# Order of the steps within a scan chunk, and the queue of the last group's norm, in a two-layer gated-MLP and state-space decoder

## The chip, the cores and the metric

One Trainium2 chip; the program runs on one core. The core has five engines with a queue each, worked off in order: TensorE (PE; its weight loads are shown as PEld), VectorE (DVE), ScalarE (ACT), GpSimd (POOL) and SyncE (SP), which only issues DMAs. ScalarE and GpSimd can issue DMAs from their own queues as well. Engines wait for each other through semaphores, and an instruction that waits holds all that stand behind it in its queue. The metric is the device time of one execution in microseconds, less is better.

## What is computed

Two layers on 1024 tokens of width 1024, in float32. Layer 0 is a chunked causal spatial-gating MLP, layer 1 a Mamba-2 mixer with 8 groups, 4 heads each, and chunks of 128 tokens. Only layer 1 matters here:

```python
def ssd_mixer(h, w_in, conv_w, conv_b, dt_bias, a_log, d_skip, norm_w, w_out):
    proj = h @ w_in                                  # z, x, B, C, dt
    xbc = silu(causal_depthwise_conv(xbc, conv_w, conv_b))        # 4 taps along tokens
    dt = softplus(dt_raw + dt_bias); dA_cs = cumsum(dt * -exp(a_log), axis=2)   # inside a chunk
    decay = exp(where(causal, dA_cs[l] - dA_cs[s], -inf))
    w_ls = einsum('bclgn,bcsgn->bclsg', Cm, Bm)[..., None] * decay * dt
    y_diag = einsum('bclsgj,bcsgjp->bclgjp', w_ls, x)             # inside a chunk
    states = einsum('bclgn,bclgj,bclgjp->bcgjpn', Bm, decay_to_end * dt, x)
    prev = scan(lambda carry, s: carry * chunk_decay + s)         # from chunk to chunk
    y = y_diag + einsum(Cm, prev, exp(dA_cs)) + x * d_skip
    gated = rmsnorm_per_group(y * silu(z), norm_w)                # over 256 channels of a group
    return gated @ w_out
# h = h + ssd_mixer(rmsnorm(h)); out = rmsnorm(h, final_norm_w)
```

## The kernel before

Large matrix products are done by a seven-product scheme (products 1 to 7 of half-size blocks), each operand split into a high and a low part so that three matmuls (`mm3`, L134 to L136) make one precise one. ScalarE makes the high part (a cast, L111), VectorE or GpSimd the low part (L112).

**The scan** (`scans`) walks over 64 chunks in the order of groups, eight of each group. Of chunk c, class `Scan` has these steps:

- `load` (SyncE): the running decays of the chunk. `decay` (ScalarE): four Relu and one Exp make the decay matrix in tile `wl` (L1544, L1546).
- `pe_a` (TensorE): transposes of x and B and the product of B and C, into the PSUM tile `tp`. `tokens`: VectorE scales x (L1552) and masks the product (L1554), ScalarE copies B (L1556, behind VectorE's two), GpSimd makes the weighted x (L1557).
- `weights` (VectorE, L1562): decay matrix times the masked product, in `wl`.
- `pe_b` (TensorE): the chunk's output `yy` (L1571 with `wl`, L1575 with the state) and its contribution `sp` to the state (L1582).
- `update` (VectorE, L1601): the state takes `sp` in. `out` (VectorE L1613, L1616, GpSimd L1619): the output is assembled. `carry` (GpSimd, L1592): the next state is decayed. `gate` (GpSimd, L1623): times silu(z).

The loop runs these staggered: in turn n it does `pe_b`, `update`, `out`, `gate` of chunk n, `weights` and `carry` of n+1, `pe_a`, `decay`, `tokens` of n+2 and `load` of n+3. PSUM tiles `tp`, `yy` and `sp` share four buffers in turn.

Between `pe_b` and `pe_a`, and at the end of the turn, `project` lets TensorE do a unit or more of other work: the input projections of groups 2, 4, 6 and 7 (PSUM tile `ab`, two buffers), then z of group 7, and from the last chunks on the first of the output products (`bo`). A finished projection puts its convolution into `queue`: a ScalarE step (L1287) and three taps on VectorE (L1281) which read `ab`, then Silu; `drain()` takes one entry per turn, and all but the newest are drained before another accumulator is taken. GpSimd makes the low part of the projections' weights (L112).

**The output product** (`bo`, class `Out`) takes its inner order 1, 2, 7, 6, 4, 5, 3. The gated outputs of groups 0 to 6 come back from DRAM (`ya<-g_d`, L1696) and are scaled with the norm's 1/rms (`rb`, read back as a broadcast, L1688; the scaling is L1701, called `ready`); group 7 stays on chip. `prep` splits the operands of one of four steps c. `hook_b(n, c)` is called ahead of the matmuls of product n, step c, and issues loads and the VectorE operations between the products. In the scan's last seven chunks `ready` and `prep` of product 1 come at the head of each turn.

**The norm of a group**: squares on ScalarE (L1634), a sum on GpSimd (L1641), row sums on TensorE (L1647), a copy (L1651), a store `sum_c` (L1654), a read-back as columns (`sv`, L1663), the inverse root in three parts `guess` (L1667, L141), `tail` (L150 to L153) and `put` (a store, L1676), and then the broadcast read `rb`. For the last group this is done by halves of the tokens (`end["half"]`). The DMAs of all groups go by SyncE's queue but for those of the last group, and `put` and `rb` of the last two, which go by ScalarE's.

All is scheduled by hand: the order of the program is the order in each queue. DMAs of SyncE and ScalarE use nine completion semaphores in turn.

Of the kernel before, what the change touches and what calls it, by code (L numbers as in the profile page):

```python
# [15 lines left out]
P = 128  # L16
# [6 lines left out]
G = 8  # L23
# [6 lines left out]
def kernel(  # L30
# [21 lines left out]
    nc = tc.nc  # L52
    x = x[0]
    out = out[0]
# [497 lines left out]
    for gp in range(G // 2):  # L552
# [4 lines left out]
        if gp == 1:  # L557
# [9 lines left out]
            for h in range(2):  # L567
# [9 lines left out]
                for k in range(4):  # L577
                    g = h * 4 + k
# [79 lines left out]
    class Out:  # L658
# [111 lines left out]
        def get(self, kind, i, k, c):  # L770

            at = kind, i, k, c if kind == "a" else c // 2
            if at not in self.had:
                self.had.add(at)
                (self.load_a if kind == "a" else self.load_b)(*at[1:])
# [569 lines left out]
    queue = []  # L1345

    def drain(n=1):

        for _ in range(min(n, len(queue))):
            for f in queue.pop(0):  # L1350
                f()
# [139 lines left out]
    ss_d = dr.tile([G, T], F32, name="ss_d")  # L1491
    rs_d = dr.tile([G, T], F32, name="rs_d")
# [16 lines left out]
    class Scan:  # L1509
# [141 lines left out]
                nc.scalar.copy(out=self.sr[h * 64:h * 64 + 1], in_=pr[h * 64:h * 64 + 1, 0:256])  # L1651

        def sum_c(self, th):
            (nc.sync if self.g < G - 1 else nc.scalar).dma_start(out=ss_d[self.g, th * 512:(th + 1) * 512].rearrange("(h t) -> h t", h=2),  # L1654
                              in_=self.sr[0:65:64])

    def group_rstd(g, t0, n):


        c = n // P  # L1660
        sv = tiny([P, 8], "sv")[:, 0:c]
        queue = nc.sync if g < G - 1 else nc.scalar
        queue.dma_start(out=sv, in_=ss_d[g, t0:t0 + n].rearrange("(p c) -> p c", c=c))  # L1663
        got = []

        def guess():
            nc.vector.tensor_scalar(sv, sv, 1.0 / 256, NORM_EPS, ALU.mult, ALU.add)  # L1667
            got.append(rsqrt_a(sv, c))

        def tail():  # L1670
            rv = tiny([P, 8], "rvv")[:, 0:c]
            rsqrt_b(rv, sv, got[0], c)
            got.append(rv)

        def put():
            (nc.sync if g < G - 2 else nc.scalar).dma_start(out=rs_d[g, t0:t0 + n].rearrange("(p c) -> p c", c=c), in_=got[1])  # L1676

        return guess, tail, put

# [3 lines left out]
    def weights(g, th):  # L1683

        if (g, th) not in rbs:
            n = min(2 - g % 2, G - 1 - g) or 1
            t = q4([P, 2, 512], "rb")
            (nc.sync if g < G - 2 else nc.scalar).dma_start(out=t[:, 0:n], in_=rs_d[g:g + n, th * 512:(th + 1) * 512].partition_broadcast(P))  # L1688
            for k in range(n):
                rbs[g + k, th] = t[:, k]  # L1690
        return rbs[g, th]
# [15 lines left out]
    def accs_b(n):  # L1707
        if n == 1:
# [3 lines left out]
    bo = Out(gd, b_w_out, gscale, lambda t, nb: h1_d[t][:, nb * 512:(nb + 1) * 512], accs_b, False,  # L1712
             (1, 2, 7, 6, 4, 5, 3))
    end = {}

    def hook_b(n, c):

        last, get = end["scan"], bo.get
        at = n, c
        if at == (1, 0):  # L1720
            for k in (2, 3):
                get("a", 0, 0, k)
            get("b", 0, 0, 2)
        elif at == (1, 2):
            for k in (0, 1):
                get("a", 0, 1, k)
            get("b", 1, 0, 0)
        elif at == (1, 3):
            end["half"] = [group_rstd(G - 1, 0, 512)]
            get("a", 0, 1, 2), get("b", 1, 0, 2)  # L1730
            for k in (0, 1):
                get("a", 1, 0, k)
            get("b", 0, 1, 0)
            end["half"][0][0]()
            last.sum_b(n=2)
        elif n == 2:
            if c == 0:
                last.sum_c(1)
                for k in (2, 3):
                    get("a", 1, 0, k)  # L1740
                get("b", 0, 1, 2)
                end["half"][0][1]()
            elif c == 1:
                end["half"][0][2]()
                end["half"].append(group_rstd(G - 1, 512, 512))
                get("a", 1, 1, 0), get("a", 1, 1, 1)
                get("a", 0, 1, 3)
                end["half"][1][0]()
            elif c == 2:
                end["half"][1][1]()  # L1750
            elif c == 3:
                end["half"][1][2]()
                bo.ready(1, 1, 0)
            if c < 2:
                bo.b12_plus(1, c)
            bo.ready(1, 0, c)
            bo.plus(bo.a(0, 0, c), bo.a(1, 0, c))
        elif n == 7:
            if c == 0:
                get("a", 1, 1, 2), get("a", 1, 1, 3)  # L1760
            if c < 3:
                bo.ready(1, 1, c + 1)
                bo.sums(2, c)
        elif n == 6:
            if c == 0:
                bo.sums(2, 3)
            bo.sums(6, c)
            if c % 2 == 0:
                get("b12", 0, 1, c)
            if c == 0:  # L1770
                end["fnwb"] = q4([P, D], "fnwb")
# [31 lines left out]
    def scans():  # L1803
# [13 lines left out]
        def project(upto):  # L1817
            while ran[0] < upto:
                next(fl, None)
                ran[0] += 1  # L1820

        def want(at):
            if at < M:
                return AHEAD + (total - AHEAD) * at // M
            return total + min(16 * (at - M) // (N - 5 - M), 16 + 2 * (at - N + 5))

        def at(f, n, *a):
            if 0 <= n < N:
                g, c = chunks[n]
                if g not in scan:  # L1830
                    scan[g] = Scan(g, nc.gpsimd)
                getattr(scan[g], f)(c, *a)
# [16 lines left out]
        for n, (g, c) in enumerate(chunks):  # L1849
            if n == M + 3:  # L1850
                drain(len(queue))
            elif n == N - 9:
                for k in range(2):
                    bo.get("a", 0, 0, k)
            elif n == N - 7:
                end["scan"] = scan[G - 1]
                bo.get("b", 0, 0, 0)
            if n >= N - 7:
                k = n - N + 7
                if k % 2:  # L1860
                    bo.prep(1, k // 2)
                else:
                    bo.ready(0, 0, k // 2)
            p = g if c >= 4 else g - 1
            at("pe_b", n, scan[p] if c % 4 == 3 and p >= 0 else None)
            project(want(n + .5))
            at("pe_a", n + 2)
            at("update", n)
            at("out", n)
            if n > 0:  # L1870
                at("weights", n + 1)
            at("decay", n + 2)
            at("carry", n + 1)
            at("tokens", n + 2)
            at("gate", n)
            drain()
            at("load", n + 3)
            th = 0 if c >= 4 else 1
            if p >= 0:
                sc = scan[p]  # L1880
                if p == G - 1:
                    if c == 5:
                        sc.gate_half(th), sc.squares(th)
                    elif c == 6:
                        sc.sum_a()
                elif c % 4 == 0:
                    sc.squares(th)
                elif c % 4 == 1:
                    sc.store(th)
                    sc.sum_a()  # L1890
            if c % 4 == 0 and n >= 8:
                scan[g - 1].sum_c(1 - th)
            if g > 0:
                if c == 5:
                    rs[g] = group_rstd(g - 1, 0, T)
                elif c == 6:
                    rs[g][0]()
                elif c == 7:
                    rs[g][1]()
            if c == 0 and g > 1:  # L1900
                rs[g - 1][2]()
            if c == 1:
                prefetch(g, 1)
            if c == 5 and g < G - 1:
                prefetch(g + 1, 0)
            project(want(n + 1))
        sc = scan[G - 1]
        sc.sum_c(0), rs[G - 1][2]()
        sc.gate_half(1), sc.squares(1)
        for _ in fl:  # L1910
            pass

# [51 lines left out]
```

## Time and profile before

| | |
|---|---|
| median of 3 runs | 1591.79 us (1590.07 to 1592.04) |
| profiled execution | 1599.45 us, its span 1597.6 us |
| mean granted clock of TensorE | 0.975 |
| busy share of the span | PE 94%, VectorE 67%, ScalarE 49%, GpSimd 26% |
| scan: first and last yy | 1071.5 us, 1425.2 us |

The profile is of one execution. A row of an order in time gives start, duration, engine, line, operation, tiles written and read, and in brackets how long the engine was idle before it and what ended the wait. `SPq` and `ACTq` rows are issues of DMAs. Waits are summed as "engine, tile, line <- what ended the wait: sum, times, longest". Weight loads and matmuls overlap, so the same wait of TensorE is a little longer when seen at the weight loads.

### The profile page before, as it was taken

The page shows a single profiled execution, that of the slowest core. Times are in us where ns is not written, and L with a number is a line of the kernel's source. Part 1 is how long each engine was busy: PE and PEld are TensorE (multiplying, and loading weights), DVE is VectorE, ACT ScalarE, POOL GpSimd, SP SyncE. Part 2 cuts the span into 40 slices and gives each one's busy share as a digit, 9 for nine tenths or more (in the row PEclk, how much of TensorE's full clock was granted, in tenths as well). Part 3 has the DMA queues.
Part 4 walks back from the last instruction along what each step waited for, and adds up shares of the span by engine and source line. Part 5 has one row for each costly group of instructions (what it writes and reads, how often), then busy time and mean ns, then how long its engine had stood idle before and what let it go on. Part 6 is the DMA issues. An engine that isn't in the chain of part 4 may idle for free.

```text
span 1597.6 us, 21214 instructions
## 1 busy us (share of the span) xinstructions
PE 1503.3 (94%) x7830; PEld 1239.6 (78%) x7830; DVE 1063.6 (67%) x1701; ACT 782.9 (49%) x1251; POOL 420.2 (26%) x441
## 2 busy tenths in 40 slices
PE   5799999999999999998999999989999999987997
PEld 4799988888888887776788787767777777766876
DVE  7976566666666644777737377646776666777876
ACT  4522232332323354655555555546666666755363
POOL 3601110000000131210011312116766666532121
PEclk8899999999999999999999999999999999998999
DMA  5154323322333999856367878666566464677872
GB/s 174 41 174 143 106 98 111 111 98 98 110 110 111 329 262 245 191 128 139 99 159 178 165 165 158 162 188 188 162 180 179 133 183 126 198 270 167 221 139 105
DMA packets 174839, 251.82 MB, mean 158 GB/s; under 512 B 16288, under 2 KB 102928, under 8 KB 171536
## 3 DMA queue, kind: packets, MB, share of 16 engines
q1 hardware_dynamic: 124120, 168.39, 33.9%
q0 software_dynamic: 39520, 63.19, 20.5%
q10 hardware_dynamic: 11096, 18.90, 3.3%
q8 instruction: 62, 1.02, 0.3%
q14 instruction: 41, 0.34, 0.1%
HBM read 185.61 MB, written 51.18 MB: 148 GB/s over the span
## 4 chain that ended last, share of the span: by engine, by line
PE 59%; issue 15%; DVE 10%; ACT 7%; DMA 6%; POOL 1%; SPq 1%; ACTq 1%; POOLq 0%; DVEq 0%
PE acc L136 10%; PE acc L134 9%; PE acc L135 9%; PE ab L134 4%; PE ab L136 4%; PE ab L135 4%; PE yy L1571 2%; PE yy L1575 2%; DVE wl L112 2%; PE bo L135 2%; PE bo L134 2%; PE bo L136 2%; PE ao L134 2%; PE ao L135 2%; PE ao L136 2%
## 5 line engine op out<-in xcount | busy, mean ns | idle before, releaser
L134 PE MATMUL acc<-hh,wh 128*128 128x512 f32 x868 | 343.2, 395 | 15.0 <-ACT u L292 7.2
L136 PE MATMUL acc<-hh,wl 128*128 128x512 f32 x868 | 341.7, 394 | 2.2 <-DVE wl L112 2.1
L135 PE MATMUL acc<-hl,wh 128*128 128x512 f32 x868 | 340.2, 392 | 0.0
L134 PEld LDWEIGHTS acc<-hh,wh 128*128 128x128 f32 x868 | 164.6, 190 | 51.9 <-ACT u L292 8.9
L112 DVE TENSOR_TENSOR wl<-wr,wh 128x1024 fp32r<-128x1024 f32 (+1 forms) x97 | 115.6, 1193 | 125.8 <-ACT wh L111 125.8
L136 PEld LDWEIGHTS acc<-hh,wl 128*128 128x128 f32 x868 | 164.5, 189 | 39.9 <-DVE wl L112 5.5
L135 PEld LDWEIGHTS acc<-hl,wh 128*128 128x128 f32 x868 | 164.5, 190 | 33.4
L111 ACT CAST wh<-wr 128x1024 fp32r<-128x1024 f32 (+1 forms) x113 | 116.5, 1031 | 103.1 <-PE acc L135 56.7
L292 ACT COPY u<-acc 128x512 f32<-128x512 f32 x117 | 67.7, 583 | 200.1 <-PE acc L136 198.5
L136 PE MATMUL acc<-wh,hl 128*128 128x256 f32 x448 | 131.7, 294 | 12.4 <-DVE hl L395 12.4
L134 PE MATMUL ab<-hh,wh 128*128 128x512 f32 x288 | 129.5, 450 | 7.2 <-DVE x L1281 3.8
L134 PE MATMUL acc<-wh,hh 128*128 128x256 f32 x448 | 132.5, 296 | 3.8 <-DVE vt L331 2.1
L135 PE MATMUL acc<-wl,hh 128*128 128x256 f32 x448 | 130.9, 292 | 1.3 <-DVE wl L405 1.3
L135 PE MATMUL ab<-hl,wh 128*128 128x512 f32 x288 | 114.3, 397 | 3.2 <-DVE hl L112 3.2
L136 PE MATMUL ab<-hh,wl 128*128 128x512 f32 x288 | 115.2, 400 | 0.0
L136 PEld LDWEIGHTS acc<-wh,hl 128*128 128x128 f32 x448 | 90.2, 201 | 13.5 <-DVE hl L395 13.5
L134 PEld LDWEIGHTS acc<-wh,hh 128*128 128x128 f32 x448 | 90.4, 202 | 4.8 <-ACT wh L111 2.3
L135 PEld LDWEIGHTS acc<-wl,hh 128*128 128x128 f32 x448 | 90.5, 202 | 1.7 <-DVE wl L405 1.5
L134 PE MATMUL bo<-wh,xh 128*128 128x512 f32 x192 | 78.5, 409 | 8.0 <-ACT wh L111 7.2
L112 DVE TENSOR_TENSOR xl<-ya,xh 128x1024 fp32r<-128x1024 f32 x40 | 49.9, 1246 | 53.1 <-ACT xh L111 53.1
L1544 ACT ACTIVATE wl<-wl,tk 128x128 f32<-128x128 f32 x256 | 81.5, 391 | 0.6 <-DMA wl<-cs_d 0.3
L645 POOL DMA_DIRECT2D y_d<-y x8 | 4.4, 548 | 290.9 <-DVE y L642 290.9
(320 smaller groups left out, 3284.0 us busy)
## 6 DMA issues: line engine op xcount, KB each, us to landing
wr<-in_a_w_in_dram SPq DMA_DIRECT2D x48, 512.0 KB, 3.8
wl<-cs_d SPq DMA_DIRECT2D x64, 256.0 KB, 3.4
wr<-in_b_w_in_dram SPq DMA_DIRECT2D x30, 512.0 KB, 5.1
wb<-in_a_w_out_dram SPq DMA_DIRECT2D x10, 1024.0 KB, 11.2
wb<-in_b_w_out_dram SPq DMA_DIRECT2D x10, 1024.0 KB, 8.0
wr<-in_b_w_in_dram SPq DMA_DIRECT2D x36, 256.0 KB, 5.7
v<-v_d SPq DMA_DIRECT2D x8, 1024.0 KB, 5.0
y_d<-y POOLq DMA_DIRECT2D x8, 1024.0 KB, 5.6
```

Of the source, the lines that this page charges most:

```text
L111: nc.scalar.copy(out=hi, in_=src)
L112: return (eng or nc.vector).tensor_tensor(out=lo, in0=src, in1=hi.bitcast(F32), op=ALU.subtract)
L134: nc.tensor.matmul(out=o, lhsT=l[0], rhs=r[0], start=start, stop=False, **kw)
L135: nc.tensor.matmul(out=o, lhsT=l[0], rhs=r[1], start=False, stop=False, **kw)
L136: nc.tensor.matmul(out=o, lhsT=l[1], rhs=r[0], start=False, stop=stop, **kw)
L292: nc.scalar.copy(out=self.u[n][:, i], in_=a)
L645: store = lambda: nc.gpsimd.dma_start(out=y_d[-1], in_=y)
L1544: nc.scalar.activation(wl[:, j, :], wl[:, j, :], AF.Relu, scale=-1.0, bias=tokc(2, c, self.g)[:, j:j + 1])
L1571: nc.tensor.matmul(out=yy[f * 64:(f + 1) * 64, pt * P:(pt + 1) * P], lhsT=w[:, j * 64:(j + 1) * 64], rhs=wl[:, j, :], start=True, stop=True)
L1575: nc.tensor.matmul(out=yy[:, 256 + pt * P:384 + pt * P], lhsT=self.state[c - 1][:, pt * P:(pt + 1) * P], rhs=self.x(3, c), start=True, sto ...
```

## The change

In a turn of the scan `weights` of chunk n+1 goes ahead of `update` and `out` of n; `drain` goes ahead of `tokens`; `ready` and `prep` of product 1 go from the head of the turn to its end. All DMAs of the norm of the last two groups go by SyncE. The loads of the second quarter (`a` 0, 1 and `b` 1, 0) are asked for at the scan's end, and the last group's first half is read back there; `guess`, `tail` and `put` of that half come one to two steps earlier in the product; `guess` and `tail` of the second half come one step later, its read-back one step earlier; the load of its last part (`a` 0, 1, 3) comes one step earlier.

```diff
         def sum_c(self, th):
-            (nc.sync if self.g < G - 1 else nc.scalar).dma_start(out=ss_d[...], in_=self.sr[0:65:64])
+            nc.sync.dma_start(out=ss_d[...], in_=self.sr[0:65:64])
...
     def group_rstd(g, t0, n):
-        queue = nc.sync if g < G - 1 else nc.scalar
-        queue.dma_start(out=sv, in_=ss_d[g, t0:t0 + n]...)
+        nc.sync.dma_start(out=sv, in_=ss_d[g, t0:t0 + n]...)
...
         def put():
-            (nc.sync if g < G - 2 else nc.scalar).dma_start(out=rs_d[...], in_=got[1])
+            nc.sync.dma_start(out=rs_d[...], in_=got[1])
...
     def weights(g, th):
-            (nc.sync if g < G - 2 else nc.scalar).dma_start(out=t[:, 0:n], in_=rs_d[...])
+            nc.sync.dma_start(out=t[:, 0:n], in_=rs_d[...])
...
     def hook_b(n, c):
         elif at == (1, 2):
-            for k in (0, 1):
-                get("a", 0, 1, k)
-            get("b", 1, 0, 0)
+            end["half"][0][0]()
         elif at == (1, 3):
-            end["half"] = [group_rstd(G - 1, 0, 512)]
             get("a", 0, 1, 2), get("b", 1, 0, 2)
+            end["half"][0][1](), end["half"][0][2]()
             for k in (0, 1):
                 get("a", 1, 0, k)
             get("b", 0, 1, 0)
-            end["half"][0][0]()
             last.sum_b(n=2)
         elif n == 2:
             if c == 0:
                 last.sum_c(1)
                 for k in (2, 3):
                     get("a", 1, 0, k)
+                get("a", 0, 1, 3)
                 get("b", 0, 1, 2)
-                end["half"][0][1]()
+                end["half"].append(group_rstd(G - 1, 512, 512))
             elif c == 1:
-                end["half"][0][2]()
-                end["half"].append(group_rstd(G - 1, 512, 512))
                 get("a", 1, 1, 0), get("a", 1, 1, 1)
-                get("a", 0, 1, 3)
+            elif c == 2:
                 end["half"][1][0]()
-            elif c == 2:
-                end["half"][1][1]()
             elif c == 3:
-                end["half"][1][2]()
+                end["half"][1][1](), end["half"][1][2]()
                 bo.ready(1, 1, 0)
...
     def scans():
         for n, (g, c) in enumerate(chunks):
...
-            if n >= N - 7:
-                (prep or ready, as below)
             p = g if c >= 4 else g - 1
             at("pe_b", n, scan[p] if c % 4 == 3 and p >= 0 else None)
             project(want(n + .5))
             at("pe_a", n + 2)
+            if n > 0:
+                at("weights", n + 1)
             at("update", n)
             at("out", n)
-            if n > 0:
-                at("weights", n + 1)
             at("decay", n + 2)
             at("carry", n + 1)
+            drain()
             at("tokens", n + 2)
             at("gate", n)
-            drain()
+            if n >= N - 7:
+                k = n - N + 7
+                if k % 2:
+                    bo.prep(1, k // 2)
+                else:
+                    bo.ready(0, 0, k // 2)
             at("load", n + 3)
...
         sc = scan[G - 1]
+        for k in (0, 1):
+            bo.get("a", 0, 1, k)
+        bo.get("b", 1, 0, 0)
         sc.sum_c(0), rs[G - 1][2]()
         sc.gate_half(1), sc.squares(1)
+        end["half"] = [group_rstd(G - 1, 0, 512)]
```

More of the change, by code (lines that the diff above doesn't have):

```diff
@@ L1653, in sum_c @@
         def sum_c(self, th):
-            (nc.sync if self.g < G - 1 else nc.scalar).dma_start(out=ss_d[self.g, th * 512:(th + 1) * 512].rearrange("(h t) -> h t", h=2),
+            nc.sync.dma_start(out=ss_d[self.g, th * 512:(th + 1) * 512].rearrange("(h t) -> h t", h=2),
                               in_=self.sr[0:65:64])
@@ L1661, in group_rstd @@
         sv = tiny([P, 8], "sv")[:, 0:c]
-        queue = nc.sync if g < G - 1 else nc.scalar
-        queue.dma_start(out=sv, in_=ss_d[g, t0:t0 + n].rearrange("(p c) -> p c", c=c))
+        nc.sync.dma_start(out=sv, in_=ss_d[g, t0:t0 + n].rearrange("(p c) -> p c", c=c))
         got = []
@@ L1675, in put @@
         def put():
-            (nc.sync if g < G - 2 else nc.scalar).dma_start(out=rs_d[g, t0:t0 + n].rearrange("(p c) -> p c", c=c), in_=got[1])
+            nc.sync.dma_start(out=rs_d[g, t0:t0 + n].rearrange("(p c) -> p c", c=c), in_=got[1])
         return guess, tail, put
@@ L1687, in weights @@
             t = q4([P, 2, 512], "rb")
-            (nc.sync if g < G - 2 else nc.scalar).dma_start(out=t[:, 0:n], in_=rs_d[g:g + n, th * 512:(th + 1) * 512].partition_broadcast(P))
+            nc.sync.dma_start(out=t[:, 0:n], in_=rs_d[g:g + n, th * 512:(th + 1) * 512].partition_broadcast(P))
             for k in range(n):
@@ L1857, in scans @@
                 bo.get("b", 0, 0, 0)
+            p = g if c >= 4 else g - 1
+            at("pe_b", n, scan[p] if c % 4 == 3 and p >= 0 else None)
+            project(want(n + .5))
+            at("pe_a", n + 2)
+            if n > 0:
+                at("weights", n + 1)
+            at("update", n)
+            at("out", n)
+            at("decay", n + 2)
+            at("carry", n + 1)
+            drain()
+            at("tokens", n + 2)
+            at("gate", n)
             if n >= N - 7:
@@ L1863, in scans @@
                     bo.ready(0, 0, k // 2)
[L1864 to L1869, printed above, removed]
-            if n > 0:
-                at("weights", n + 1)
[L1872 to L1875, printed above, removed]
-            drain()
             at("load", n + 3)
```

## The prediction

> **What bounds the kernel now.** I read the page's head first, then busy time by stretch, then who waited for whom on TensorE in each stretch, then the order in time around the longest waits.
>
> ```profile
> span 1597.6 us, 21214 instructions
> PE 1503.3 (94%) x7830; PEld 1239.6 (78%) x7830; DVE 1063.6 (67%) x1701; ACT 782.9 (49%) x1251; POOL 420.2 (26%) x441
> ```
> ```profile
> core 0: us, PE busy (x) PEld busy (x) DVE busy (x) ACT busy (x) POOL busy (x), PEclk, DMA share, GB/s
> 1055.00:1380.00 325.00, 314.40 (x1872) 240.69 (x1871) 212.36 (x455) 207.58 (x431) 206.60 (x229) 0.99 0.57 162
> 1380.00:1428.00 48.00, 40.31 (x238) 30.09 (x237) 35.74 (x71) 30.19 (x58) 21.00 (x24) 0.95 0.78 261
> 1428.00:1470.00 42.00, 33.17 (x138) 25.23 (x138) 27.01 (x43) 21.97 (x26) 8.67 (x8) 0.91 0.69 176
> 1470.00:1598.00 128.00, 116.81 (x502) 95.04 (x500) 100.36 (x139) 61.46 (x90) 23.04 (x25) 0.97 0.65 158
> ```
>
> TensorE sets the time. The edit touches only the scan and what follows: rows one to three are the scan filled with projections, its last chunks filled with the output product, and that product's next part. TensorE is idle 10.6 (325.0 - 314.4), 7.7 and 8.8 us there. Only these idle times, and the clock, can be won. In the same order, its waits:
>
> ```profile
> PE yy L1571 <- issue: 4.7, 4, 1.8
> PE ab L134 <- DVE x L1281: 3.8, 2, 1.9
> PE ab L134 <- DVE bc L1281: 1.9, 1, 1.9
> ```
> ```profile
> PE yy L1571 <- issue: 4.0, 2, 3.3
> PE yy L1571 <- DVE wl L1562: 2.5, 1, 2.5
> PE yy L1571 <- ACT wl L1546: 0.8, 1, 0.8
> ```
> ```profile
> PE bo L134 <- ACT wh L111: 7.2, 2, 6.4
> PE bo L135 <- DVE wl L112: 1.6, 2, 0.9
> ```
>
> The columns are sum, times and longest. A chunk's matmuls (yy) wait for its weights (wl); a projection (ab) waits until the last convolution tap has emptied its accumulator; the product (bo) waits for operand splits.
>
> **The change, part by part.** No arithmetic is added or removed. Four things move.
>
> *Weighting ahead of the state's update.* One chunk on VectorE before:
>
> ```profile
> 1125.39 0.43 DVE L1601 TENSOR_TENSOR state<-sp,state 128x256 f32<-128x256 f32 x1 [1.30 <-PE sp L1582]
> 1126.58 0.69 DVE L1562 TENSOR_TENSOR wl<-wl,cw 128x512 f32<-128x512 f32 x1
> 1127.26 0.42 DVE L1552 TENSOR_TENSOR cw<-tp,tk 128x256 f32<-128x256 f32 x1
> 1127.80 1.27 DVE L1281 SCALAR_TENSOR_TENSOR bc<-ab,par,bc 128x1021 f32<-128x1021 f32 x1
> ```
>
> VectorE stood 1.30 us waiting for TensorE's sp and only then, 1.19 us on, began the weighting of the next chunk, which needs nothing of sp. Ahead of the update it fills that idle time. Where TensorE waited longest in the middle, the weighting had met a GpSimd operation:
>
> ```profile
> 1132.79 2.39 POOL L112 TENSOR_TENSOR wl<-wr,wh 128x1024 fp32r<-128x1024 f32 x1 [3.11 <-ACT wh L111]
> 1132.91 2.81 DVE L1562 TENSOR_TENSOR wl<-wl,cw 128x512 f32<-128x512 f32 x1
> ```
> ```profile
> L1562 DVE TENSOR_TENSOR wl<-wl,cw 128x512 f32<-128x512 f32 x56 | 52.4, 936 | 0.8 <-ACT wl L1546 0.7
> ```
>
> 2.81 us instead of 0.69, and TensorE waits for it. In the new place it may meet such an operation too, but has the whole of update, tap and tokens (some 3 us by the rows above) in hand. I take the 4.7 us of the middle as won. Kept back: the weighting now waits for ScalarE's exponentials ahead of the update. That wait is 0.7 us in 56 chunks, so I cost it at nothing; VectorE's idle 112.6 us in the 325 (325.0 - 212.4) hides it. With that cover gone it would cost each late exponential in full.
>
> *Convolution step ahead of the tokens.* Site 1331:
>
> ```profile
> 1331.40 0.68 DVE L1562 TENSOR_TENSOR wl<-wl,cw 128x512 f32<-128x512 f32 x1
> 1332.62 1.27 DVE L1281 SCALAR_TENSOR_TENSOR x<-ab,par,x 128x1021 f32<-128x1021 f32 x1
> ```
>
> The tap can start where the weighting stood: 1332.62 - 1331.40 = 1.22 us earlier. Three such waits of 1.9 us shrink to about 0.7: 3.7 us. The tokens come 1.27 us later; who needs them is the chunk two on, and one chunk takes 5.5 us (the 56 of the last row lie in the 310 us from 1070 to 1380). ScalarE's copy waits for the tokens and its next exponentials queue behind it; both have that chunk in hand, and the convolution's ScalarE step no longer waits behind the copy. I charge nothing; the bounds are a gain of 1.27 us per tap that ScalarE's earlier step could bring, where a tap waits for it, and a loss as in the slower rival below.
>
> *The clock.* Windows of TensorE:
>
> ```profile
> 1252.50:1255.90 3.40, 3.40 (x16) 0.50 0.95 307
> 1293.90:1297.30 3.40, 3.40 (x20) 1.00 0.00 0
> 1334.40:1337.80 3.40, 3.40 (x15) 0.51 0.00 0
> 1464.20:1474.30 10.10, 6.13 (x14) 0.50 0.98 170
> ```
>
> The column after the count is the granted clock. Two of the three tap waits were followed by 3.4 us at half clock, the third not, so 1.9 us is at the edge and 0.7 should be under it. Bounds: nothing, and half of 3.4 twice, 3.4; I take 3.0. The Trainium skill, page "TensorE: Matmul & The Clock Gate", section "What's actually happening", says that the clock falls to half after an idle window of about 3.4 us. By that rule waits of 1.9 us cost no clock, shortening them wins none, and this term would be zero; the trace shows half clock after 1.9 us, so the row decides.
>
> Middle: 4.7 + 3.7 + 3.0 = 11.4 us.
>
> *Operand splits to the end of the chunk.* The longest wait of the last chunks:
>
> ```profile
> 1407.16 1.23 DVE L112 TENSOR_TENSOR xl<-ya,xh 128x1024 fp32r<-128x1024 f32 x1 [3.66 <-ACT xh L111]
> 1411.40 0.66 PE L1571 MATMUL yy<-wl,cw 128*64 128x128 f32 x8 [3.29 <-issue]
> ```
>
> Before, the split stood ahead of update and weighting: VectorE waits 3.66 us for ScalarE's cast, and update, weighting and yy queue behind. At the end of the chunk update and weighting are through first. All three kinds of wait there, 4.0 + 2.5 + 0.8 = 7.3 us, have this form. What is late next: the last chunk's sum of squares, behind the gating of the first half, ScalarE's squares and GpSimd's add, about the 2.5 us of the last wait again. I take 5.0 (bounds 0 and 7.3).
>
> *The last norm in SyncE's queue.* The wait of 6.4 us:
>
> ```profile
> 1455.62 0.32 ACTq L1676 DMA_DIRECT2D rs_d<-rvv  x1
> 1460.59 0.33 ACTq L1688 DMA_DIRECT2D rb<-rs_d  x1
> ```
> ```profile
> 1454.36 1.22 DVE L112 TENSOR_TENSOR wl<-wb,wh 128x1024 fp32r<-128x1024 f32 x1
> ...
> 1460.78 0.17 DVE L1667 TENSOR_SCALAR sv<-sv 128x4 f32<-128x4 f32 x1 [5.20 <-DMA sv<-ss_d]
> ...
> 1462.30 1.22 DVE L748 TENSOR_TENSOR ya<-ya 128x1024 f32<-128x1024 f32 x1
> 1463.96 1.41 DVE L1701 SCALAR_TENSOR_TENSOR ya<-x,par,rb 128x512 f32<-128x512 f32 x2 [0.44 <-DMA rb<-rs_d]
> 1466.54 1.23 DVE L112 TENSOR_TENSOR xl<-ya,xh 128x1024 fp32r<-128x1024 f32 x1 [1.17 <-ACT xh L111]
> 1467.68 1.22 DVE L112 TENSOR_TENSOR wl<-wb,wh 128x1024 fp32r<-128x1024 f32 x1
> ```
>
> Before, the store of 1/rms for the first half (1455.62) sits in ScalarE's queue behind splits, its read-back follows 4.97 us later, and VectorE stands 5.20 us. After, the row sums are read back as the scan ends, the store follows two product steps earlier on SyncE, and its flight of 5 us is hidden by a step of product 2. VectorE's chain from one wl to the next is then 1.41 + 1.22 + 1.41 + 1.17 + 1.14 + 1.14 = 7.5 us (two scalings, one add, the wait for the cast, the split) against 13.3 measured (1467.68 - 1454.36): 5.8 won. What stays is VectorE's own pace. Each DMA that now waits on SyncE, the sums' store, their read-back, the store of 1/rms and the read-back of group 6, has the loads of the second half behind it; in flights of 5 us these loads come some 10 us later than before, just when VectorE's scalings want them: between nothing and one flight, 5.0; I charge the middle, 2.5. The clock row gives 10.1 us at half from 1464.2; of it TensorE works from 1467.5, so at most 3.4 can be won; I take half, 1.7. End: 5.8 - 2.5 + 1.7 = 5.0.
>
> **Sum.** 11.4 + 5.0 + 5.0 = 21.4 us off this execution, which took 1599.45 us (span 1597.6 and 1.85 around it), 7.66 above the median 1591.79. Some of the waits and half clocks above must be its own, so I take 3.4 off: 18 us from the median, 1574.
>
> **The rivals.**
>
> *The end gives nothing* (SyncE's queue becomes the wait): each wait on SyncE holds the loads of the second half; if they land 5 us later than charged, VectorE stands that long in product 2 instead of for sv. For it: VectorE already paces that product, 7.5 us a step. Against: the loads are wanted a step after the store. Time: 1574 + 5, and the tail's gain partly refilled, 1581.
>
> *Nothing net*: waits only change places, since TensorE is busy 96.7% (314.4 of 325) in the middle and a late exponential or cast can hold it as the weighting did. Time 1591.
>
> *Slower: the weighting loses to GpSimd in its new place.* It now follows the tokens, and the tokens release GpSimd's product for the state:
>
> ```profile
> 1128.39 0.61 POOL L1557 TENSOR_TENSOR cw<-cw,tk 128x256 f32<-128x256 f32 x1
> 1128.96 0.72 POOL L1623 TENSOR_TENSOR ze<-ze,cw 128x256 f32<-128x256 f32 x1
> ```
>
> These two run for 1.3 us just after the tokens. If the weighting is held through both it takes 0.69 + 1.33 = 2.0 us in every chunk. VectorE's round is then 1.19 (update to weighting) + 1.27 + 0.54 (tokens) + 2.0 + 0.5 of waking = 5.5 us, level with the 5.5 us of a chunk; the chunks that carry fewer projection matmuls are shorter (some 5.0, an estimate from the mean of 5.5) and lose about 0.5 each. 48 such chunks are 24 us, 6 more than the 18: 1598. It decides from a weighting of about 1.9 us on average. Against it: the mean now is 0.94, although it meets GpSimd's adds in the old place. The Trainium skill, page "SBUF — State Buffer", section "Who interferes with whom", states such an exclusion for a VectorE operation with two SBUF inputs, whoever issues first winning; the 2.81 us row agrees with it.
>
> **How the numbers follow.** Forecast 0.60 (own range 1563 to 1584), end gives nothing 0.18, nothing net 0.09, slower 0.13. A change of 0.2%, 3.2 us, is about what a measurement of this kernel can tell from none. The first two are faster by more than that, 0.78 in all. Low end: all waits listed, 10.4 + 7.3 + 8.8, less the 2.5 that comes back and the pace kept, with the clock's 6.8 is 28 to 32 us: 1560. High end: up to the case of no change, 1592, which leaves the slower case and a little below outside.
>
> **What would show it.** Right: in the middle no yy wait over 0.5 us, ab waits under 1 us, a granted clock of 1.00 near 1252 and 1334; the last eight chunks some 5 us shorter; no 4 us hole of ScalarE or VectorE behind a norm's DMA; bo's wait of 6.4 under 2. Wrong: a mean weighting over 1.5 us, tokens that TensorE waits for, or VectorE waiting for ya or rb in product 2.

## The result, and the profile after

The changed kernel takes 1574.67 us (median of 4 runs, 1573.85 to 1575.59), the kernel before beside it 1591.91 (1590.07 to 1596.30): ratio 0.9888, 95% interval 0.9867 to 0.9909. The forecast was 1574, with 1560 to 1592 as the range. Two more groups of runs gave 0.9884 (0.9866 to 0.9901) and 0.9887 (0.9870 to 0.9904).

The profiled execution after took 1575.59 us. Head of its page, then busy time by stretch (columns as in the prediction: length, busy time of PE, PEld, DVE, ACT and POOL, granted clock, DMA share, GB/s):

```profile
span 1573.6 us, 21263 instructions
PE 1495.9 (95%) x7830; PEld 1232.2 (78%) x7830; DVE 1069.7 (68%) x1701; ACT 782.7 (50%) x1251; POOL 419.5 (27%) x441
```
```profile
1055.00:1368.00 313.00, 310.96 (x1875) 238.64 (x1873) 219.59 (x458) 209.63 (x436) 208.33 (x231) 1.00 0.62 168
1368.00:1412.00 44.00, 40.28 (x233) 29.60 (x232) 37.21 (x74) 28.03 (x54) 19.98 (x23) 0.93 0.71 240
1412.00:1455.00 43.00, 40.04 (x173) 31.03 (x172) 34.09 (x47) 25.37 (x27) 9.02 (x8) 0.99 0.88 237
```

TensorE idles 2.0 us in the middle (313.00 - 310.96), where it was 10.6, and the granted clock there is 1.00. What it still waits for, in the middle, in the last chunks, and in the products 1, 2 and 7 (in rows of `bo`, `xh` and `wh` are the high parts of the product's operands, `xl` and `wl` the low parts; in rows of `yy`, `wl` is the chunk's weights):

```profile
PE ab L134 <- DVE x L1281: 1.1, 2, 0.7
PE sp L1647 <- POOL gsq L1641: 0.5, 1, 0.5
PE yy L1571 <- issue: 0.4, 1, 0.4
```
```profile
PE sp L1647 <- POOL gsq L1641: 2.8, 1, 2.8
PE bo L135 <- DVE wl L112: 0.8, 1, 0.8
```
```profile
PE bo L135 <- DVE wl L112: 3.6, 4, 1.1
PE bo L134 <- ACT wh L111: 1.1, 2, 0.6
```

The yy waits of 4.7 and 7.3 us are down to 0.4, the tap waits are 0.7 at most, the wait of 6.4 is 0.6. In their place stand one wait of 2.8 (0.3 before) for the last group's sum of squares, and a row of small ones of the product for wl.

Where the time went is read best from five landmarks in the order of TensorE's weight loads: the first yy, the 57th (chunk 0 of group 7), the last, the first load of product 2 and the first of product 6. Before, then after:

```profile
1071.55 0.42 PEld L1571 LDWEIGHTS yy<-wl,cw 128*64 128x64 f32 x8
1382.57 0.42 PEld L1571 LDWEIGHTS yy<-wl,cw 128*64 128x64 f32 x8 [0.35 <-ACT cw L1556]
1424.94 0.45 PEld L1571 LDWEIGHTS yy<-wl,cw 128*64 128x64 f32 x8 [2.91 <-issue]
1442.06 0.19 PEld L134 LDWEIGHTS bo<-wh,xh 128*128 128x128 f32 x1
1498.38 0.19 PEld L134 LDWEIGHTS bo<-wh,xh 128*128 128x128 f32 x1
```
```profile
1069.40 0.42 PEld L1571 LDWEIGHTS yy<-wl,cw 128*64 128x64 f32 x8
1368.26 0.42 PEld L1571 LDWEIGHTS yy<-wl,cw 128*64 128x64 f32 x8 [0.35 <-issue]
1402.90 0.45 PEld L1571 LDWEIGHTS yy<-wl,cw 128*64 128x64 f32 x8 [0.50 <-PE bo L136]
1423.58 0.19 PEld L134 LDWEIGHTS bo<-wh,xh 128*128 128x128 f32 x1
1474.53 0.19 PEld L134 LDWEIGHTS bo<-wh,xh 128*128 128x128 f32 x1 [0.86 <-issue]
```

The differences of neighbours, for these two and for the profiled executions of the experiments below (us):

| kernel | first to 57th yy | 57th to last | last yy to product 2 | products 2 and 7 | first yy to the end |
|---|---|---|---|---|---|
| before | 311.0 | 42.4 | 17.1 | 56.3 | 526.1 |
| after, three executions | 298.9, 299.2, 298.9 | 34.6 | 20.7, 19.6, 20.8 | 51.0, 51.7, 51.4 | 504.2, 504.3, 504.8 |
| weighting put back | 308.0 | 35.7 | 18.3 | 51.4 | 512.4 |
| tap put back | 306.2 | 35.3 | 20.9 | 51.2 | 512.6 |
| splits put back | 298.9 | 39.0 | 20.3 | 48.6 | 505.9 |
| norm put back | 298.8 | 34.6 | 20.7 | 54.8 | 508.3 |
| norm alone | 309.4 | 40.9 | 16.7 | 49.9 | 516.1 |
| weighting and tap alone | 299.3 | 39.0 | 20.1 | 54.4 | 512.0 |
| addition on GpSimd | 298.8 | 34.6 | 20.9 | 53.4 | 506.8 |
| sum on TensorE | 298.9 | 34.7 | 19.9 | 49.8 | 502.3 |
| scaling ahead | 300.1 | 34.6 | 19.7 | 51.1 | 504.6 |
| sum and scaling | 299.5 | 34.6 | 20.0 | 51.2 | 504.5 |

From before to after: middle -12.2, last chunks -7.7, up to product 2 +3.6, products 2 and 7 -5.4, the rest -0.2: 21.9 us in all. Another 2.2 us lie ahead of the first yy, in work that the change does not touch (1071.55 to 1069.40). The profile before stood 7.5 us above its median, the one after 0.9, hence 23.9 us between the profiled executions and 17.2 between the medians. Every row of the table but the second is one execution.

### The profile page after: what moved, and what is told of

The parts are those of the page before. It is cut to its first block, busy times and chain, and to the rows that moved or that the text cites. A ratio compares the mean times of both kernels' runs of the same rounds, so it can differ in the third digit from the quotient of the medians.

```text
span 1573.6 us, 21263 instructions
## 1 busy us (share of the span) xinstructions
PE 1495.9 (95%) x7830; PEld 1232.2 (78%) x7830; DVE 1069.7 (68%) x1701; ACT 782.7 (50%) x1251; POOL 419.5 (27%) x441
## 5 line engine op out<-in xcount | busy, mean ns | idle before, releaser
L135 PE MATMUL bo<-wl,xh 128*128 128x512 f32 x192 | 76.7, 399 | 5.8 <-DVE wl L112 5.8
## 6 DMA issues: line engine op xcount, KB each, us to landing
wr<-in_a_w_in_dram SPq DMA_DIRECT2D x48, 512.0 KB, 3.7
wr<-in_b_w_in_dram SPq DMA_DIRECT2D x30, 512.0 KB, 5.0
```

What stands on the lines that cost most here:

```text
L135: nc.tensor.matmul(out=o, lhsT=l[0], rhs=r[1], start=False, stop=False, **kw)
```

## The experiments

A difference of 3.2 us (0.2%) is about what the medians can tell; below that I go by the rows and the table. Each group of runs had the kernel before beside it.

**The changed kernel again**, beside the variants.

> The changed kernel once more, beside the variants that undo one part of it. Both theories (the parts add up; or one part carries nearly all) expect what the first runs showed, 1574 to 1576 us, some 17 us under the kernel before, TensorE idle about 2 us between 1055 and 1370 us with a granted clock of 1.00 there, and half clock for 6.8 us after the wait for the sum of squares near 1407 us. The waits that stay the same from one execution to the next belong to the order of the program, the others to the execution.

1574.72 us (1571.37 to 1577.37), ratio 0.9884. Between 1055 and 1370 us the waits are the same three rows, with the same numbers: they belong to the program's order.

**The weighting put back.**

```diff
-            if n > 0:
-                at("weights", n + 1)
             at("update", n)
             at("out", n)
+            if n > 0:
+                at("weights", n + 1)
```

> The changed kernel with the weighting alone put back behind the state's update and the output. Theory of the prediction: the yy waits of the middle come back, four waits and some 4.7 us in all, the longest about 1.8; TensorE idle between 1055 and 1370 us rises from 2.0 to about 6.7 us, and the time by 4.7, to about 1579.5. In the last chunks, where the splits stay at the end of the chunk, nothing more. Rival: the weighting was late only because other work of VectorE stood ahead of it, and with the tap and the splits moved it has time enough in either place: 1575, within 1 us, no yy wait over 0.5.

1579.52 us, 4.8 above the changed kernel beside it; ratio 0.9913 (0.9897 to 0.9928). TensorE's waits in its middle, and the weighting over 56 chunks in the changed kernel and here:

```profile
PE yy L1571 <- issue: 5.9, 4, 1.8
PE ab L134 <- DVE x L1281: 2.3, 2, 1.3
```
```profile
L1562 DVE TENSOR_TENSOR wl<-wl,cw 128x512 f32<-128x512 f32 x56 | 52.5, 937 | 15.2 <-ACT wl L1546 12.1
```
```profile
L1562 DVE TENSOR_TENSOR wl<-wl,cw 128x512 f32<-128x512 f32 x56 | 55.1, 984 | 0.4
```

The yy waits are back, and the rival (time enough in either place) is out. The profiled execution is the longest of its six, 1583.78 us: its middle takes 9.1 us more (308.0 to 298.9), with 8.9 of waits in all where 2.0 were, and with one window at half clock behind a wait of 1.7:

```profile
1224.95:1228.30 3.35, 3.35 (x11) 2.57 (x10) 2.07 (x7) 2.07 (x6) 2.68 (x4) 0.50 0.56 155
```

By the medians this part is worth 4.8 us; by the table it is worth 9.1 in the middle and 7.6 to 8.2 up to the end (512.4 for 504.2 to 504.8), with 1.7 of it for the window. In its new place the weighting waits 12.1 us for the exponentials. The prediction had taken this wait at 0.7, as it was in the old place. Still no wait of TensorE comes of it, so that the price of nothing was right: VectorE's idle time covers it.

**The tap put back.**

```diff
-            drain()
             at("tokens", n + 2)
             at("gate", n)
+            drain()
```

> The changed kernel with the convolution step alone put back behind tokens and gate. Theory of the prediction: three waits of TensorE for the last tap grow from 0.7 back to about 1.9 us, 3.7 us in all, and two of the three are followed by 3.4 us at half clock, another 3: 1578 to 1582, granted clock near 0.99 between 1055 and 1370 us. Rival: the waits return and the clock stays at 1.00, so 3.7 us and no more: 1578.5. Second rival: with the weighting already moved ahead, VectorE is early enough for the tap in the old place as well: 1575, waits under 1 us. The Trainium skill, page 'TensorE: Matmul & The Clock Gate', section 'What's actually happening', says that the clock falls to half after an idle window of about 3.4 us; by that rule waits of 1.9 us cost no clock, and the first rival would be right.

1583.14 us (1579.74 to 1587.62), 8.4 above; ratio 0.9937 (0.9919 to 0.9955). Waits in its middle, and two windows:

```profile
PE ab L134 <- DVE x L1281: 3.8, 2, 1.9
PE ab L134 <- DVE bc L1281: 1.9, 1, 1.9
```
```profile
1247.90:1251.30 3.40, 3.40 (x17) 2.41 (x15) 0.00 (x0) 3.39 (x3) 2.14 (x1) 0.50 1.06 282
1329.85:1333.25 3.40, 3.40 (x16) 2.27 (x14) 0.00 (x0) 3.39 (x3) 3.40 (x2) 0.50 0.00 0
```

The three waits of 1.9 us are back to the tenth, and two of them are again followed by 3.4 us at a clock of 0.50, as in the kernel before. The middle is 7.3 us longer (306.2 to 298.9): 4.6 of waits (5.7 to 1.1), and 2.7 left for two windows whose halves are 1.7 each. Both rivals are out. Which of the waits half clock follows changes with the execution (see *Middle* below). By the rule of the Trainium skill, page "TensorE: Matmul & The Clock Gate", section "What's actually happening", that half clock follows an idle window of about 3.4 us, these waits would have cost no clock; the rows of two kernels say otherwise.

**The splits put back.**

```diff
+            if n >= N - 7:          # ready / prep, as before
+                ...
             p = g if c >= 4 else g - 1
             ...
             at("gate", n)
-            if n >= N - 7:
-                ...
```

> The changed kernel with the operand splits of the last seven chunks alone put back to the head of the turn, ahead of the state's update and the weighting. Theory of the prediction: update and yy queue behind a split that waits for ScalarE's cast, the yy waits of the last chunks come back, 5 us in all (0 to 7.3), the middle stays as it is: about 1580. Rival: the weighting now stands ahead of the update, so it no longer queues behind it, and the split at the head costs only what the update has to spare: 1575 to 1576.

1576.08 us, 1.4 above; ratio 0.9889 (0.9872 to 0.9907). Waits in its last chunks:

```profile
PE yy L1571 <- DVE wl L1562: 3.4, 1, 3.4
PE yy L1571 <- ACT wl L1544: 2.2, 1, 2.2
PE sp L1647 <- POOL gsq L1641: 1.7, 1, 1.7
```
The mechanism is as predicted: the yy waits return, 5.6 us, and the last chunks take 4.3 us more (38.96 to 34.65). But the end gives most of it back: 1.1 less of waiting for the sum of squares, 2.4 instead of 3.6 of waiting for wl, and products 2 and 7 take 48.6 us instead of 51.0 to 51.7. As I read it, a scan that ends sooner finds VectorE's operands not ready. My theory of 5 us is wrong as the worth of this part; the rival's number is right, its reason is not, since the queueing is there.

**The norm put back** (queues, hooks and first calls of the last group's norm as before), and **the norm alone** on the kernel before.

> The changed kernel with the norm part alone undone: the loop over the chunks is the new one, queues and places of the last group's norm are those of before. Theory of the prediction: ScalarE and VectorE stand 4 to 5 us behind the DMAs of the norm again, the product waits some 6 us for a cast in its second product, with half clock behind it, and the time rises by 5.0, to about 1580. Second theory, from the sums of the undone parts so far (4.8, 8.4 and 1.4 of 17.8): about 3 us remain for this part, 1577.5 to 1578. Rival of the prediction (the end gives nothing): 1575, within 1 us, since VectorE's own pace in the products sets the end in any case.

> The kernel before with the norm part alone done: queues and places of the last group's norm are new, the loop over the chunks is the old one. If the parts add up, it gains what undoing it costs: 3 to 5 us, 1587 to 1589. If the end of the changed kernel runs at VectorE's pace, so that a scan that ends 5 us sooner gains only 1.4 (the run with the splits put back), then the norm part is worth more here than in the changed kernel: with the scan's end late, VectorE has its operands ready ahead of TensorE, no wait of the product over 1 us stays, and the gain is 5 us or more, 1587 or less.

Put back: 1577.34 us, ratio 0.9902 (0.9885 to 0.9919). Alone: 1585.30 us, 8.6 below the kernel before beside it (1593.88), ratio 0.9947 (0.9932 to 0.9962). Waits in the products with the norm put back, and with the norm alone:

```profile
PE bo L134 <- ACT wh L111: 6.3, 2, 5.3
```
```profile
PE bo L135 <- DVE wl L112: 1.6, 2, 0.9
PE bo L134 <- ACT wh L111: 0.9, 1, 0.9
```

The long wait comes back, and yet undoing costs 0.9902 - 0.9884 to 0.9888, some 2.5 us (3.5 to 4.1 by the table): the 5.0 of the prediction is out for this place, the 3 us of the second theory fit. Doing it alone gains 8.6 by the medians. Of the table's 10, 6.8 lie behind the last yy (16.7 + 49.9 for 17.1 + 56.3); the rest lies in stretches that it does not touch, 1.6 in the middle and 1.5 in the last chunks, where this execution has one window at half clock fewer each. The parts do not add up. The theory's reason fits the rows: with the scan's end late, VectorE has its operands ready, and no wait of the product over 1 us stays.

**Weighting and tap alone**, to see what the splits are worth without the new norm.

> The kernel before with weighting and tap alone moved; the splits stay at the head of the turn, the norm in its old queue and places. All theories: the middle as in the changed kernel, 12 us less between the first chunk's yy and the 57th. They part at the splits, whose worth without the new norm this run gives against the run with the norm alone undone (1577.3 there). If what the tail wins is lost again to VectorE's pace only where the norm is new, the splits are worth 5 us here, and this run takes 1582 to 1583. If most of it is lost again at the wait for the sum of squares, which needs no new norm, they are worth 2 us or less, and it takes 1579.

1581.12 us, ratio 0.9920 (0.9904 to 0.9936). Its middle takes 299.3 us, as in the changed kernel. Against the norm put back (0.9902) the splits are worth 2.9 us, by the table 3.7 (512.0 to 508.3); with the new norm 1.4, by the table 1.1 to 1.6. Between the two expectations: the wait for the sum of squares stands here too, and only the rest of the loss belongs to the new norm's company.

**What holds products 2 and 7?** VectorE's splits of the second operand in product 2 of the changed kernel; then SyncE's queue, and one scaling in product 7 that waits for its load:

```profile
1428.20 1.22 DVE L112 TENSOR_TENSOR wl<-wb,wh 128x1024 fp32r<-128x1024 f32 x1
1435.74 1.22 DVE L112 TENSOR_TENSOR wl<-wb,wh 128x1024 fp32r<-128x1024 f32 x1
1443.18 1.22 DVE L112 TENSOR_TENSOR wl<-wb,wh 128x1024 fp32r<-128x1024 f32 x1
```
```profile
1450.03 0.33 SPq L1675 DMA_DIRECT2D rs_d<-rvv  x1
1450.45 1.14 SPq L1687 DMA_DIRECT2D rb<-rs_d  x1
1451.64 0.94 SPq L1695 DMA_DIRECT2D ya<-g_d  x1
```
```profile
1463.67 1.42 DVE L1700 SCALAR_TENSOR_TENSOR ya<-ya,par,rb 128x512 f32<-128x512 f32 x2 [2.74 <-DMA ya<-g_d]
```

VectorE's step is 7.5 us (7.54, 7.44), TensorE's 5.4 (a product of four steps takes 21.8). Three edits were tried on it.

*The addition of product 2 on GpSimd.*

```diff
-            bo.plus(bo.a(0, 0, c), bo.a(1, 0, c))
+            nc.gpsimd.tensor_tensor(out=bo.a(0, 0, c), in0=bo.a(0, 0, c), in1=bo.a(1, 0, c), op=ALU.add)
```

> The changed kernel with the addition of two gated blocks in product 2 (128x1024, 1.22 us on VectorE, four times) done by GpSimd. Theory (VectorE's own pace sets products 2 and 7): its step there falls from 7.5 to about 6.3 us, the waits of 1.2 us for wl in product 2 go and those of product 7 shrink, 2 to 3.6 us, about 1572. Rival: the addition takes some 2.4 us on GpSimd (as its split of the same shape in the scan), and VectorE's scalings and splits are stretched where they meet it, as the weighting of 2.81 us was; no gain, 1575, or a loss of some 2 us.

1577.06 us, ratio 0.9895 (0.9878 to 0.9911): no gain, some 1.5 us above the changed kernel, and products 2 and 7 at 53.4. The order in time on VectorE, then on GpSimd, and TensorE's waits:

```profile
1431.42 4.18 DVE L112 TENSOR_TENSOR xl<-ya,xh 128x1024 fp32r<-128x1024 f32 x1 [1.20 <-ACT xh L111]
```
```profile
1431.62 2.89 POOL L1750 TENSOR_TENSOR ya<-ya 128x1024 f32<-128x1024 f32 x1
```
```profile
PE bo L135 <- DVE wl L112: 7.4, 3, 3.4
```

A split of 1.22 us takes 4.18 beside an addition of 2.89: 2.96 more, the whole of it. The rival was right. The rows show that the two hold each other up, not which of them goes first: VectorE's starts 0.20 us ahead of GpSimd's. The Trainium skill, page "SBUF — State Buffer", section "Who interferes with whom", says that a VectorE operation with two SBUF inputs contends with a GpSimd operation that reads SBUF; the row of 4.18 us agrees.

*The sum of squares of the last group's first half wholly on TensorE.*

```diff
-                ends.sum_b(sp[:, 256:512])
+                ends.sum_b(sp[:, 256:512], 2 if ends.g == G - 1 else 1)
 ...
-                    elif c == 6:
-                        sc.sum_a()
```

> The changed kernel with the sum of squares of the last group's first half done wholly by TensorE (two more matmuls' worth of columns, as for the second half), without GpSimd's addition. Theory A (the wait of 2.8 us near 1407 and the half clock behind it are a loss of their own): both go, 3 to 4.5 us, about 1571. Theory B (the end runs at VectorE's pace): TensorE comes 3 us sooner to product 2 and waits there for wl instead, as the run with the splits put back showed the other way round; 0 to 1.5 us, 1573.5 to 1575, with waits of the product in products 2 and 7 longer by 2 us in sum.

1572.67 us, ratio 0.9870 (0.9852 to 0.9889); by the table 2.0 to 2.5 us less from the first yy on. The wait of 2.8 us is gone, and the product still waits 3.7 us for wl.

Neither theory exactly: more comes through than the 1.5 of B, less than the 3 of A.

*The scaling that the next split needs, ahead of the other scaling and the addition*, and *both*. With the first, the changed kernel once more.

```diff
+            if c < 2:
+                bo.ready(0, 1, c + 2)
             bo.ready(1, 0, c)
             bo.plus(bo.a(0, 0, c), bo.a(1, 0, c))
```

(and `bo.ready(0, 1, 1)` at the end of product 1, step 3)

> The changed kernel beside the next three. 1574 to 1576 us; from the last chunk's yy to the end 170.4 to 170.8 us, as in its two executions so far, with two half products of product 2 (12 and 14 us) and two of product 7 (11.8 and 13) above the 10.9 that TensorE needs.

> The changed kernel with the scaling that product 2's next split needs put ahead of the scaling and the addition for product 7, in the four steps where it stood behind them. Nothing else moves. Theory (VectorE's chain paces product 2: 1.41 + 1.22 + 1.41 + 1.17 of waiting for ScalarE's cast + 1.14 + 1.14): the cast now runs beside the other scaling and the addition, VectorE's wait of 1.17 goes, its step falls from 7.5 to about 6.3 us in two or three steps, 2.3 to 3.5 us, some of it kept in product 7 as well: 1570 to 1573. Rival (the operands' loads and the broadcast of 1/rms come only just in time): the scaling stands 5 us earlier than now and waits for them, and all behind it: no gain, 1575 or some us more.

> The changed kernel with both: the scaling ahead, and the sum of squares of the last group's first half wholly on TensorE without GpSimd's addition. If VectorE's pace behind the scan and the wait for the sum are two losses in a row, the gains stand on each other: TensorE comes sooner to product 2 and VectorE follows, 2.2 (measured alone) + 2.3 to 3.5, and up to 2 more of what the pace took back from the first: 1567 to 1571. If the pace takes back all that the first brings, 1570 to 1573 as with the order alone.

The changed kernel 1576.33 us (0.9887), scaling ahead 1572.21 (0.9868, 0.9849 to 0.9886), both 1575.16 (0.9880, 0.9863 to 0.9897). VectorE with the scaling ahead, then its wait for the load of ya:

```profile
1427.79 1.22 DVE L112 TENSOR_TENSOR wl<-wb,wh 128x1024 fp32r<-128x1024 f32 x1
...
1434.03 1.22 DVE L112 TENSOR_TENSOR wl<-wb,wh 128x1024 fp32r<-128x1024 f32 x1
1436.28 1.41 DVE L1700 SCALAR_TENSOR_TENSOR ya<-x,par,rb 128x512 f32<-128x512 f32 x2 [1.03 <-DMA rb<-rs_d]
```
```profile
DVE ya L1700 <- DMA ya<-g_d: 3.0, 1, 3.0
```

The step falls from 7.5 to 6.24 us (1434.03 - 1427.79), as the theory says; the next one waits 1.03 us for the broadcast of 1/rms, and in product 7 the load of ya holds VectorE 3.0 us. With both, these waits are 1.2 and 3.5. Products 2 and 7 stay at 51.1 and 51.2. The medians of the two kernels, 4.1 us below and 1.2 below, do not fit a common gain, their intervals overlap that of the changed kernel, and the table shows next to none: from the last yy to product 6 they take 70.8 and 71.2 us, the changed kernel 71.3 to 72.2. (Its third execution takes 171.3 us from the last yy to the end, where I had expected 170.4 to 170.8, so that differences of this size are near its own spread.) No gain is shown. The median with the scaling ahead lies in the range of its theory, but the rows are those of the rival: VectorE's pace and the loads in SyncE's queue end within some 3 us of each other, and speeding up the one hands the time to the other. Both expectations for the two edits together, 1567 to 1571 and 1570 to 1573, were too low; its execution also has 3.4 us at half clock in product 7 (1468.55 to 1471.95), some 1.7 of loss.

No version that clearly beats the changed kernel came out; the sum on TensorE is the best candidate, 2 us below by the rows of one execution, and it did not show on top of the scaling ahead (504.5 to 504.6). Issuing the load of ya ahead of the store of 1/rms was not tried.

## Why the prediction came out right, step by step

*Middle.* Forecast 11.4, table 12.2. TensorE's waits fall by 8.6 us (10.6 to 2.0), which the forecast had at 4.7 + 3.7; the rest is the two windows at half clock, 1.7 each. The waits belong to the program's order, the windows to the execution. The norm alone runs the old loop and shows the old waits to the tenth, 4.7 for yy and 5.7 for the tap, but only one window at half clock behind the taps, at the site that had none in the kernel before. The stretches behind its three tap waits (length, busy time of PE, granted clock, DMA share, GB/s):

```profile
1247.20:1257.20 10.00, 10.00 (x60) 1.00 1.01 260
1288.10:1291.45 3.35, 3.35 (x12) 0.50 0.00 0
1329.60:1339.60 10.00, 10.00 (x61) 1.00 0.09 30
```

Its middle takes 309.4 us, so that against this execution the change gains 10.5. The clock's 3.0 was thus read from one execution; in this other one of the same loop it is worth 1.7. Of the parts put back, the weighting's 4.7 came out at 4.8 by medians and 9.1 by the table, tap and clock together, 6.7, at 8.4 and 7.3. By medians the two undone one at a time (13.2) and done together (0.9920, 12.7 us) agree within the 3 us that medians can tell. By the table they do not: 16.4 one at a time, 11.7 together (311.0 - 299.3), since the weighting put back brings longer yy waits than before (5.9 for 4.7) and longer tap waits too (2.5 for 1.1). That the two terms simply add up is not shown.

*Tail.* Forecast 5.0, with the sum of squares late next at about 2.5. The wait is 2.8, and up to product 2 the change gains 7.7 - 3.6 = 4.1. (The last chunks of the norm alone, with the old loop and a granted clock of 1.00 for 0.96, take 40.9; against them the 7.7 is 6.3.) What the working left out is the half clock behind that wait:

```profile
1405.95:1412.75 6.80, 5.68 (x15) 3.86 (x16) 6.67 (x12) 0.73 (x2) 3.76 (x3) 0.50 0.01 1
```

and that VectorE does not follow. The kernel before has as much at half clock there (1412.95 to 1416.30 and 1426.60 to 1430.00 at 0.50), which the working does not count either, so that the two largely cancel. As a part of the sum the term was near; as the worth of moving the splits it is mis-sized, 1.4 instead of 5.0.

*End.* Forecast 5.0, products 2 and 7 gain 5.4. The step of VectorE came out as worked out, 7.5 us, and the half clock is gone: the granted clock is 1.00 from 1423.60 to 1474.50. One reading was off: the 5.20 us of VectorE are the wait for the second half's row sums, whose read-back stood in ScalarE's queue right behind the store that the prediction names:

```profile
1456.04 0.45 ACTq L1663 DMA_DIRECT2D sv<-ss_d  x1
```

The 2.5 charged for loads behind SyncE's waits was there in size and in another place: not in product 2, where VectorE waited for no load, but in product 7, 2.74 us (2.5 and 3.4 in the other two executions). There the load of ya (issued at 1451.64) stands in SyncE's queue behind the store of the second half's 1/rms (1450.03), which waits for VectorE. Before, this queue was free, and the last three loads of ya were out more than a product ahead of their use:

```profile
1444.98 2.08 SPq L1696 DMA_DIRECT2D ya<-g_d  x3
```

*What was taken off for the execution.* 3.4 us; it was 6.6 (23.86 between the profiled executions, 17.24 between medians), and the true sum was 21.9 + 2.2 rather than 21.4. The two misses, 3.2 and 2.7, nearly cancel: that the median lies 0.7 us from the forecast is luck. Of the 6.6, the norm alone names 3.1: the windows at half clock that its execution has fewer in the middle and the last chunks.

*The rivals.* The slower one needed a mean weighting of 1.9 us; it is 0.937, as before (0.936). The 0.5 us of waking in its sum stands in no row: where VectorE waits for another engine in the kernel before, between 1055 and 1500 us, it starts at most 0.11 us after that engine's instruction ends. "The end gives nothing" and "nothing net" are out by the runs with the norm and with weighting and tap alone. The mechanism of the first, a load behind SyncE's waits, is real, at half its price.

*What would show it.* yy 0.4 us in the middle (0.5 forecast), tap waits 0.7, clock 1.00, the last eight chunks 7.7 shorter (5), the longest wait of VectorE for a norm's or the product's DMA 2.7 (no hole of 4), the wait of 6.4 now 0.6 (under 2).

## What to carry to other kernels

Where the bounding engine waits in a fixed order of program, the same tap waits came back to the tenth of a microsecond in three kernels; move the instruction that is waited for ahead of one that itself waits, and take the gain from the wait's row. Half clock read from one profile is that execution's, and makes a range, not a value. Gains ahead of a stretch where a second engine keeps pace need not be worth their rows: here, what the scan won at its end was lost again for one half and more where VectorE had no lead. A store that waits, put into the queue that also carries loads, held up the load after it here, one product later than where I had looked.

## What had not been expected of the hardware

The wait of 2.8 us for the sum of squares was followed by 3.4 to 6.8 us at half clock in the changed kernel's three executions, and where it was 6.8 the stretch up to product 2 took 1.1 us more (20.7 and 20.8 against 19.6). The prediction put the edge near a wait of 1.9 us. In the norm alone half clock also followed two waits of 0.9 us, 0.86 at 1446.67 and 0.95 at 1448.12, while two of 1.90 in the same execution were not followed by it, so that the length of the single wait does not decide:

```profile
1448.50:1451.90 3.40, 3.40 (x10) 0.50 1.12 262
```

In the middle of the changed kernel, with waits of 0.7 us at most, none of its three executions has any. The load of one ya tile took 11.9 us from issue to landing in the DMA view between 1440 and 1470 us, when the engines of the DMA were busy nearly throughout:

```profile
ya<-g_d SPq DMA_DIRECT2D x1, 512.0 KB, 11.9
```

The prediction had used flights of 5 us, those of the small stores.
